# S5 local response from Toeplitz tables spread by one-hot matmuls, 28 adaLN weight tiles moved to VectorE, z from turned u on

## The chip, the cores and the metric

The kernel runs on one core of one Trainium2 chip. Its engines run side by side, each with its own queue in order: TensorE (PE: matmul, with PEld for its weight loads), VectorE (DVE), ScalarE (ACT), GpSimd (POOL) and SyncE (SP), which issues most DMAs. The metric is the device time of one execution in microseconds. Before the change three runs gave a median of 1373.99 us (1372.52 to 1379.91).

## The reference, cut to what matters

The program is a decoder trunk of two layers on 256 tokens of width 2048. Layer 0 is an S5 state-space layer, layer 1 a native-sparse-attention layer on shared keys and values. Each layer is normalised and modulated by shift, scale and gate that come from a vector c (adaLN).

```python
c_act = jax.nn.silu(c)
shift, scale, gate = jnp.split(c_act @ mod_w[layer] + mod_b[layer], 3, axis=-1)
h = modulate(rmsnorm(x, norm_g[layer]), shift, scale)
# S5 mixer, 128 groups of 16 channels and 64 complex states
u, z = jnp.split(h @ w_in, 2, axis=-1)
x_t = a * x_{t-1} + bb @ u_t            # diagonal, complex, over 256 steps
y = Re(c @ x) + d_skip * u
y = gelu(y); y = y * sigmoid(y @ w_glu + b_glu)
out = (y * silu(z)) @ w_out
```

The scan is done in blocks of 4 steps. What a step of a block gives to later steps of the same block (four 16x16 matrices per group, K_0 to K_3, and the d_skip diagonal) is the local response; what crosses blocks goes through the states.

## The kernel before

Everything stays transposed, with channels on the 128 partitions. A projection of one 128-column block reads 1 MB of weights in two tiles of 512 KB (ring of 8 buffers, `raw`). ACT rounds four 128-column pieces at a time to a high part (`hi`, L203), DVE takes the low part by subtraction (`lo`, L204), and PE makes three 256-column matmuls for each piece (L228 to L230): 48 to a block.

adaLN columns are made in two ways. A PE pair (`pe_mod_pair`, L158 and L163) takes two 128-column blocks with 32 matmuls of 32 output rows and a small sum; `dve_mod` (L145) takes one block as two 512 KB tiles, each by one DVE multiply with accumulate of 128x1024, against `cact`, the row silu(c) laid on all partitions. `PE_MODS` and `DVE_MODS` say which columns go where: 32 to PE, 64 to DVE (beside 32 for the first shift and scale, always on PE).

The program runs in stages:

- the first norm, half of u (L299 to L302) with the first adaLN columns, and, on DVE, the discretised tables of the S5 layer;
- the S5 stage, in halves f = 0 and 1 of the groups: `u_turn` (L544) brings u from channel order to group order, `scan_in` (L597) forms the block inputs, `scan_run` (L622 to L644) runs the scan on DVE, `scan_out` (L657) forms the outputs from the states, `y_turn` turns back (L672) and adds the local response (L679) by 32x32 matmuls with `kd`, then ACT takes the gelu. u's second half and z are projected meanwhile. z overwrites x0, which holds u until y_turn has read it (the assert in `z_half`);
- glu and w_out, then the second norm (hkv), the projections of keys and values with the compressed blocks, the rows of q;
- 16 attention heads, each with its z, w_o, and the last norm.

Every call of `fill()` takes the next entry of the table `PLAN`; its letters say what is put there: u or z half blocks (`u`, `z`), a PE pair (`m`), a DVE column (`d`), compressed pieces and q rows (`c`, `q`). A scheduler then orders each engine's instructions by its own estimate of times.

Of the kernel before, what the change touches and what calls it, by code (L numbers as in the profile page):

```python
# [46 lines left out]
def spread(n, slots, a=0):  # L47
# [25 lines left out]
def trunk_kernel(ctx, tc, xT, crow, ccol, vec, m0n, mn, mt, w_ur, w_in, w_glu, w_out, w_kv, w_qr, w_q, w_g,  # L73
# [49 lines left out]
    kd = ey[:, 0:2048].rearrange("p (m d c) -> p m d c", m=16, d=4)  # L123
# [10 lines left out]
    modw = pool.tile([128, 80], F32, name="modw")  # L134
# [3 lines left out]
    def dve_mod(n=1):  # L138
        for i in range(ndve[0], min(ndve[0] + n, len(DVE_MODS))):
            col = DVE_MODS[i]  # L140
            for e in range(2):
# [5 lines left out]
                                               accum_out=modw[:, col - 48:col - 47] if e else modv[:, col:col + 1])  # L147
# [280 lines left out]
    V.tensor_reduce(par, id32.rearrange("p (e c) -> p e c", e=2), axis=AX.X, op=OP.add)  # L428

# [16 lines left out]
    for s in (2, 3, 0, 1):  # L446
# [14 lines left out]
        bb = [ey[:, 2112 + 256 * r:2368 + 256 * r] for r in range(2)]  # L461
# [61 lines left out]
    powers()  # L523
    pick = stab[:, 832:1104]
# [27 lines left out]

    ustate, zstate, ydone = [0, None], [0, None], [0]
# [12 lines left out]
    def z_half():  # L566
# [3 lines left out]
        assert m < 8 * ydone[0]  # L570
# [74 lines left out]

    def scan_out(f, cts):

        VH = VV[f]
        for q in range(2):
# [10 lines left out]
            for g2 in range(2):  # L660
                nc.scalar.activation(U[:, 8 * f + 4 * q:8 * f + 4 * q + 4, 2 * g2:2 * g2 + 2, :], p[g2], AF.Copy)
# [4 lines left out]
    def y_turn(f):  # L666

        for mp in range(4 * f, 4 * f + 4):
            p = psb([128, 2, 8, 4, 8], "yt")
            for j in range(4):  # L670
                for g in range(4):
                    nc.tensor.matmul(p[32 * g:32 * g + 32, :, :, j, :], turn[:, 32 * j:32 * j + 32],  # L672
                                     U[:, 2 * mp:2 * mp + 2, g, :].rearrange("p m (i s) -> p m i s", i=8),
                                     start=(j == 0), stop=False, skip_group_check=True)
            for ml in range(2):
                for d in range(4):
                    for g in range(4):
                        pr = slice(32 * g, 32 * g + 32)
# [12 lines left out]
    for q in range(4):  # L691
        fill()
# [449 lines left out]
```

## Time and profile before

| | us |
|---|---|
| median of three runs | 1373.99 |
| profiled execution | 1384.57 |
| its span, first to last instruction | 1382.9 |
| PE busy in it | 1286.8 |
| DVE busy in it | 1021.4 |
| ACT busy in it | 678.4 |
| S5 stage, from the first `ut` matmul (165.3) to the first glu matmul (437.5) | 272.2 |
| glu and w_out (437.5 to 631.5) | 194.0 |

The trace is one execution, slower by 0.8% than the median of the runs. Matmul ends are modelled, so two starts in a row tell a matmul's price better than its duration does. An idle engine costs something only where another waits for it.

### The profile page before, as it was taken

The numbers are of one execution on the slowest core, as the hardware profiler recorded it, in microseconds if no ns is written. First come the engines' busy times: TensorE is split into PE (matmuls) and PEld (weight loads), VectorE is DVE, ScalarE is ACT, GpSimd is POOL, SyncE is SP. The second block draws the span as 40 slices with busy tenths as digits, with TensorE's granted clock in tenths as the row PEclk, the third lists the DMA queues.
The fourth block names the chain that finished last, engine by engine and source line by source line (L and its number), as shares of the span: only waits on it lengthen the run. The fifth ranks groups of instructions, "written<-read, shape, count | busy, mean of one in ns | idle before, by whom it ended". The sixth has DMA issues, their size and how long they took to land.

```text
span 1382.9 us, 32898 instructions
## 1 busy us (share of the span) xinstructions
PE 1286.8 (93%) x13194; PEld 1222.9 (88%) x13194; DVE 1021.4 (74%) x2228; ACT 678.4 (49%) x1473; POOL 18.2 (1%) x44
## 2 busy tenths in 40 slices
PE   2799999889999999996999899999999999999995
PEld 1688798879889999995899899999999999999995
DVE  5998649874246888878997787777878777777665
ACT  3345543244345555543554545554565555555653
POOL 2000000000010000000000000000000000000000
PEclk9789999889999999997999999999999999999998
DMA  9798856669577899876788788876556444445541
GB/s 338 267 361 302 309 182 246 235 256 335 182 272 249 300 326 332 308 243 221 258 317 279 253 265 271 300 265 226 182 182 209 152 146 150 153 138 167 178 160 61
DMA packets 93258, 331.13 MB, mean 239 GB/s; under 512 B 12512, under 2 KB 12672, under 8 KB 92080
## 3 DMA queue, kind: packets, MB, share of 16 engines
q1 hardware_dynamic: 91792, 321.45, 67.4%
q0 software_dynamic: 1312, 7.58, 1.5%
q8 instruction: 103, 1.69, 0.5%
q14 instruction: 51, 0.42, 0.1%
HBM read 324.79 MB, written 4.19 MB: 238 GB/s over the span
## 4 chain that ended last, share of the span: by engine, by line
PE 74%; DVE 11%; DMA 11%; issue 2%; ACT 2%; SPq 0%; DVEq 0%; ACTq 0%
PE acc L230 19%; PE acc L228 18%; PE acc L229 18%; DMA raw<-in_mt_dram 8%; DVE lo L204 3%; PE macc L158 3%; DMA raw<-in_w_in_dram 2%; PE yt L679 1%; DVE raw L145 1%; PE s L976 1%; DMA mraw<-in_m0n_dram 1%; PE vp L597 1%; PE ut L544 1%; PE op L1027 1%; PE kp L473 1%
## 5 line engine op out<-in xcount | busy, mean ns | idle before, releaser
L203 ACT ACTIVATE hi<-raw 128x512 fp32r<-128x512 f32 x640 | 399.3, 630 | 425.7 <-PE acc L229 352.6
L204 DVE TENSOR_TENSOR lo<-raw,hi 128x512 fp32r<-128x512 f32 x640 | 431.8, 688 | 188.5 <-ACT hi L203 172.4
L229 PE MATMUL acc<-hq,hi 128*128 128x256 f32 x960 | 274.6, 286 | 0.0
L228 PE MATMUL acc<-hq,hi 128*128 128x256 f32 x960 | 272.9, 284 | 0.4 <-ACT hi L203 0.4
L230 PE MATMUL acc<-hq,lo 128*128 128x256 f32 x960 | 271.0, 284 | 1.8 <-DVE lo L204 1.7
L145 DVE SCALAR_TENSOR_TENSOR raw<-raw,cact 128x1024 f32<-128x1024 f32 x128 | 156.3, 1221 | 64.5 <-DMA raw<-in_mt_dram 64.3
L229 PEld LDWEIGHTS acc<-hq,hi 128*128 128x128 f32 x960 | 180.8, 188 | 3.7 <-issue 3.3
L230 PEld LDWEIGHTS acc<-hq,lo 128*128 128x128 f32 x960 | 180.3, 188 | 4.3 <-DVE lo L204 2.9
L228 PEld LDWEIGHTS acc<-hq,hi 128*128 128x128 f32 x960 | 180.9, 188 | 1.3 <-issue 0.7
L230 PE MATMUL acc<-hkv,lo 128*128 128x256 f32 x384 | 113.5, 297 | 4.1 <-DVE lo L204 3.9
L228 PE MATMUL acc<-hkv,hi 128*128 128x256 f32 x384 | 112.3, 294 | 3.5 <-ACT hkv L262 3.4
L229 PE MATMUL acc<-hkv,hi 128*128 128x256 f32 x384 | 111.2, 292 | 3.7 <-DVE hkv L263 3.7
L230 PE MATMUL acc<-h,lo 128*128 128x256 f32 x384 | 109.1, 284 | 0.2 <-DVE lo L204 0.2
L228 PE MATMUL acc<-h,hi 128*128 128x256 f32 x384 | 109.2, 284 | 0.0
L229 PE MATMUL acc<-h,hi 128*128 128x256 f32 x384 | 108.2, 282 | 0.0
L158 PE MATMUL macc<-mraw,cz 128*32 128x128 f32 x2048 | 73.1, 299 | 24.8 <-DMA mraw<-in_m0n_dram 20.1
L158 PEld LDWEIGHTS macc<-mraw,cz 128*32 128x32 f32 x2048 | 60.6, 120 | 31.7 <-issue 20.0
L230 PEld LDWEIGHTS acc<-hkv,lo 128*128 128x128 f32 x384 | 76.5, 200 | 6.3 <-DVE lo L204 6.0
L228 PEld LDWEIGHTS acc<-hkv,hi 128*128 128x128 f32 x384 | 76.7, 200 | 4.8 <-ACT hkv L262 4.6
L229 PEld LDWEIGHTS acc<-hkv,hi 128*128 128x128 f32 x384 | 76.3, 199 | 4.4 <-DVE hkv L263 4.3
L230 PE MATMUL acc<-yhl,lo 128*128 128x256 f32 x256 | 73.2, 288 | 3.4 <-DVE lo L204 3.2
L230 PE MATMUL acc<-ghl,lo 128*128 128x256 f32 x256 | 72.2, 283 | 3.3 <-DVE lo L204 3.3
(324 smaller groups left out, 2831.4 us busy)
## 6 DMA issues: line engine op xcount, KB each, us to landing
raw<-in_mt_dram SPq DMA_DIRECT2D x128, 512.0 KB, 5.4
raw<-in_w_z_dram SPq DMA_DIRECT2D x96, 512.0 KB, 3.6
mraw<-in_m0n_dram SPq DMA_DIRECT2D x64, 512.0 KB, 8.1
mraw<-in_mn_dram SPq DMA_DIRECT2D x64, 512.0 KB, 6.8
raw<-in_w_in_dram SPq DMA_DIRECT2D x48, 512.0 KB, 7.7
raw<-in_w_kv_dram SPq DMA_DIRECT2D x48, 512.0 KB, 5.4
raw<-in_w_glu_dram SPq DMA_DIRECT2D x32, 512.0 KB, 6.0
raw<-in_w_out_dram SPq DMA_DIRECT2D x32, 512.0 KB, 5.6
```

What stands on the lines that cost most here:

```text
L145: nc.vector.scalar_tensor_tensor(out=rf, in0=rf, scalar=1.0, in1=cact[:, 1024 * e:1024 * e + 1024], op0=OP.mult, op1=OP.mult, accum_out=mo ...
L158: nc.tensor.matmul(acc[32 * j:32 * j + 32, 128 * e:128 * e + 128], cz[:, q, :], r[:, q % 8, :], start=(e == 0 and q < 4), stop=(q >= 12), ...
L203: nc.scalar.activation(hi[:, 0:c, :], rr, AF.Copy)
L204: nc.vector.tensor_sub(lo[:, 0:c, :], rr, hi[:, 0:c, :].bitcast(F32))
L228: nc.tensor.matmul(acc, hi[:, kk, :], act(0, k), start=(k == 0), stop=False)
L229: nc.tensor.matmul(acc, hi[:, kk, :], act(1, k), start=False, stop=False)
L230: nc.tensor.matmul(acc, lo[:, kk, :], act(0, k), start=False, stop=(k == KT - 1))
L473: nc.tensor.matmul(kp[o:o + 32, x].rearrange("p b m -> p (b m)"), bb[r][pr, 32 * h:32 * h + 32], kc_[pr, 2 * h:2 * h + 2, r, :], start=(x ...
L544: nc.tensor.matmul(p[o:o + 32].rearrange("p m (i s) -> p m i s", i=8), pick[:, i:i + 32], ucm[:, bs, :, j, :], start=(j % 2 == 0), stop=(j ...
L597: nc.tensor.matmul(p[e][64 * g2:64 * g2 + 64, hl, r, :], VH[pr, r, h].rearrange("p b m -> p (b m)")[:, 64 * g2:64 * g2 + 64], U[pr, 8 * f ...
L679: nc.tensor.matmul(p[pr, ml, :, d:4, :], kd[pr, 2 * mp + ml, d, :], ucm[pr, 2 * mp + ml, :, 0:4 - d, :], start=False, stop=(d == 3), skip_ ...
L976: nc.tensor.matmul(sp, qo(a, h)[:, qs], kk[:, kv, b, o:o + w], start=(i == 0), stop=(i == 2))
```

## The change

`kd` becomes `kdt`, a quarter of its size in columns: each 32 partitions hold a group pair's [K_0..K_3] as 64 columns (the ACT copies for two parities become one ACT copy and one DVE multiply-add). In the new `scan_local(f)` matmuls of K=32 and M=128 with a shifted one-hot matrix `sel` spread them to block-Toeplitz tables in PSUM, ACT copies those to `tz`, and 64x64 matmuls apply them to the group-ordered u in place (`U`). `scan_out` adds the states' part to U with DVE instead of copying with ACT; `y_turn` only turns. u in channel order is then read by `u_turn` alone, so z may begin once both halves are turned. `scan_out(0)` stands ahead of `scan_run(1)`. `cact` is loaded right after the power tables, into `ey`, over `bb`. 14 columns (28 tiles) go from `PE_MODS` to `DVE_MODS`; columns 32 to 47, the first gate, are now the first of DVE's. `PLAN` is new.

```diff
-NA, NB = 16, 0
-PE_MODS = list(range(32, 48)) + list(range(96, 96 + NA)) + L1[:NB]
-DVE_MODS = list(range(96 + NA, 128)) + L1[NB:] + list(range(80, 96))
+NA, NB = 10, 8
+PE_MODS = list(range(96, 96 + NA)) + L1[:NB]
+DVE_MODS = list(range(32, 48)) + list(range(96 + NA, 128)) + L1[NB:] + list(range(80, 96))
...
-    "uu", "uu", "muu", "uu", "muu", "uu", "muu", "uu", "m", "", "m", "",
+    "ud", "ud", "ud", "ud", "uu", "uu", "uuuud", "uuuudd", "zd", "z", "zd", "z", "z", "z", "zz", "zz",
...
-        for e in range(2):
-            nc.scalar.activation(kd[:, 4 * s:4 * s + 4, :, 16 * e:16 * e + 16], ...
+        kx = kdt[s // 2][:, 4 * (s % 2):4 * (s % 2) + 4]
+        nc.scalar.activation(kx, kp[:, :, 0], AF.Copy, scale=par[:, 0:1])
+        V.scalar_tensor_tensor(kx, in0=kp[:, :, 1], scalar=par[:, 1:2], in1=kx, op0=OP.mult, op1=OP.add)
...
     powers()
+    nc.gpsimd.dma_start(cact, crow.to_broadcast((128, D)))
+    nc.scalar.activation(cact, cact, AF.Silu)
...
-        assert m < 8 * ydone[0]
+        assert m < 8 * turned[0]
...
+    def scan_local(f):
+        bs = slice(8 * f, 8 * f + 8)
+        kt = kdt[f].rearrange("p m (d c) -> p m d c", d=4)
+        for g2 in range(2):
+            for hl in range(2):
+                pr = slice(64 * g2 + 32 * hl, 64 * g2 + 32 * hl + 32)
+                p = psb([128, 8, 4, 16], "tzp")
+                for j in range(4):
+                    nc.tensor.matmul(p[:, :, j:4, :], sel[pr, 48 - 16 * j:176 - 16 * j], kt[pr, :, 0:4 - j, :],
+                                     start=(j == 0), stop=(j == 3), skip_group_check=True)
+                nc.scalar.activation(tz[:, hl], p.rearrange("p m j c -> p m (j c)"), AF.Copy)
+            for hl in range(2):
+                p = psb([128, 8, 64], "tp")
+                for m in range(8):
+                    for e in range(2):
+                        pr = slice(64 * e, 64 * e + 64)
+                        nc.tensor.matmul(p[pr, m, :], tz[pr, hl, m, :], U[pr, 8 * f + m, 2 * g2 + hl, :],
+                                         start=(m == 0), stop=True, skip_group_check=True)
+                nc.scalar.activation(U[:, bs, 2 * g2 + hl, :], p, AF.Copy)
+            fill()
...
-                nc.scalar.activation(U[:, 8 * f + 4 * q:8 * f + 4 * q + 4, 2 * g2:2 * g2 + 2, :], p[g2], AF.Copy)
+                V.tensor_add(u, u, p[g2])
...
-            for ml in range(2):
-                for d in range(4):
-                    for g in range(4):
-                        nc.tensor.matmul(p[pr, ml, :, d:4, :], kd[pr, 2 * mp + ml, d, :], ucm[pr, 2 * mp + ml, :, 0:4 - d, :], ...
...
     scan_in(0)
     scan_run(0)
-    for q in range(4):
-        fill()
+    scan_local(0)
...
     scan_in(1)
+    scan_out(0, load_ct(0))
     scan_run(1)
-    scan_out(0, load_ct(0))
+    scan_local(1)
     y_turn(0)
```

What PE does about the time of the second scan, before the change: outputs of the first half (`yp`, L657) between adaLN pairs (`macc`, L158 and L163), and then the turn (`yt`).

```order
L158 MATMUL macc<-mraw,cz 32x128 x32
L657 MATMUL yp_3466<-Vva,ctA 64x64 x15
L163 MATMUL macc<-ones,msum 128x1 x2
L657 MATMUL yp_3466<-Vva,ctA 64x64 x16
L158 MATMUL macc<-mraw,cz 32x128 x32
L657 MATMUL yp_3466<-Vva,ctA 64x64
```

The same place now: the outputs (L692 here) stand between half blocks of z (L228 to L230).

```order
L692 MATMUL yp_3363<-Vva,ctA 64x64 x32
L228 MATMUL acc<-h_160,hi 128x256
L229 MATMUL acc<-h_160,hi 128x256
L230 MATMUL acc<-h_160,lo 128x256
L228 MATMUL acc<-h_160,hi 128x256
```

24 projection matmuls of z follow each such pair of outputs where adaLN pairs stood; the spread matmuls of `scan_local(1)` (L668) come next, again between projections.

On DVE, the last part of the first scan (the fix-ups L643 and L644) stood alone before the change:

```order
L643 TENSOR_TENSOR scr<-scr 128x896
L644 TENSOR_TENSOR Vva<-Vva,scr 128x16x56
L643 TENSOR_TENSOR scr<-scr 128x896
L644 TENSOR_TENSOR Vva<-Vva,scr 128x16x56
L643 TENSOR_TENSOR scr<-scr 128x896
```

Now adaLN products (L145) and low parts for u's second half (L204) stand between them (L655 and L656 are the fix-ups).

```order
L655 TENSOR_TENSOR scr<-scr,stab 128x896
L204 TENSOR_TENSOR lo<-raw,hi 128x512 x2
L145 SCALAR_TENSOR_TENSOR raw,modv<-raw,ey 128x1024
L204 TENSOR_TENSOR lo<-raw,hi 128x512
L145 SCALAR_TENSOR_TENSOR raw,modw<-raw,ey 128x1024
L656 TENSOR_TENSOR Vva<-Vva,scr 128x16x56
```

Eight such products stand between the start of the first scan and u's last low part, and 13 between the start of the second scan and the last addition of L697.

On PE at the second norm (`rsum`, L250), the first projection of keys and values (`hkv`) followed at once:

```order
L230 MATMUL acc<-ghl_5721,lo 128x256
L250 MATMUL rsum<-tot,ones 128x256
L228 MATMUL acc<-hkv_8239,hi 128x256
L229 MATMUL acc<-hkv_8239,hi 128x256
L230 MATMUL acc<-hkv_8239,lo 128x256
```

Now four adaLN pairs stand about the norm.

```order
L230 MATMUL acc<-ghl_5122,lo 128x256
L158 MATMUL macc<-mraw,cz 32x128 x32
L250 MATMUL rsum<-tot,ones 128x256
L163 MATMUL macc<-ones,msum 128x1 x2
L158 MATMUL macc<-mraw,cz 32x128 x32
L163 MATMUL macc<-ones,msum 128x1 x2
```

Two more pairs follow, and then the same projection.

## Rows read from the trace of the kernel before

**Rows 1.** The page: busy time of each engine; the chain's shares.
```profile
PE 1286.8 (93%) x13194; PEld 1222.9 (88%) x13194; DVE 1021.4 (74%) x2228; ACT 678.4 (49%) x1473; POOL 18.2 (1%) x44
PE 74%; DVE 11%; DMA 11%; issue 2%; ACT 2%; SPq 0%; DVEq 0%; ACTq 0%
```

**Rows 2.** Windows by stage: length, busy by engine, granted clock, DMA share, GB/s.
```profile
165.30:197.30 32.00, 32.00 (x507) 25.86 (x507) 7.19 (x13) 14.81 (x36) 0.00 (x0) 1.00 0.47 159
...
254.10:297.40 43.30, 36.65 (x816) 31.80 (x811) 41.83 (x72) 12.65 (x31) 1.06 (x2) 0.76 0.64 233
297.40:356.80 59.40, 59.17 (x728) 56.68 (x718) 25.49 (x46) 24.46 (x53) 0.00 (x0) 1.00 0.91 336
...
165.30:437.50 272.20, 259.88 (x4125) 234.24 (x4125) 158.51 (x279) 111.91 (x243) 4.62 (x16) 0.94 0.68 239
...
437.50:631.50 194.00, 187.30 (x1538) 184.26 (x1537) 158.22 (x300) 99.06 (x179) 0.00 (x0) 1.00 0.86 302
631.50:663.00 31.50, 18.38 (x106) 15.83 (x105) 28.79 (x65) 12.10 (x26) 0.00 (x0) 0.73 0.55 186
663.00:857.00 194.00, 183.61 (x1461) 178.86 (x1461) 157.19 (x307) 95.95 (x186) 0.00 (x0) 0.96 0.82 275
```

**Rows 3.** Windows of 25 us: early, and one of projections alone.
```profile
75.00:100.00 25.00, 23.04 (x320) 19.37 (x313) 24.97 (x35) 11.06 (x26) 0.56 (x1) 0.87 1.00 384
...
575.00:600.00 25.00, 25.00 (x213) 25.00 (x212) 19.56 (x38) 12.93 (x23) 0.00 (x0) 1.00 0.76 250
```

**Rows 4.** Timeline of PE: start, duration, line, shape, instructions (two records each).
```profile
165.33 7.10 PE L544 MATMUL ut<-x,stab 128*32 128x512 f32 x64
...
194.29 1.91 PE L597 MATMUL vp<-U,Vva 64*64 64x64 f32 x64
196.12 0.39 PE L228 MATMUL acc<-h,hi 128*128 128x256 f32 x1
...
293.12 1.08 PE L672 MATMUL yt<-U,stab 128*32 128x128 f32 x32
294.13 2.38 PE L679 MATMUL yt<-x,ey 32*32 32x256 f32 x64
296.44 1.96 PE L158 MATMUL macc<-mraw,cz 128*32 128x128 f32 x64
```

**Rows 5.** The chain in order of time: outputs of the second half.
```profile
356.86 7.09 PE yp L657 x250
```

**Rows 6.** The costliest groups: adaLN on PE and on DVE.
```profile
L158 PE MATMUL macc<-mraw,cz 128*32 128x128 f32 x2048 | 73.1, 299 | 24.8 <-DMA mraw<-in_m0n_dram 20.1
L145 DVE SCALAR_TENSOR_TENSOR raw<-raw,cact 128x1024 f32<-128x1024 f32 x128 | 156.3, 1221 | 64.5 <-DMA raw<-in_mt_dram 64.3
```

**Rows 7.** Timeline of DVE: the first scan's start, two low parts, the second scan.
```profile
197.35 0.69 DVE L622 TENSOR_TENSOR scr<-Vva,scr 128x512 f32<-128x512 f32 x1 [1.72 <-ACT Vva L603]
...
199.17 0.68 DVE L204 TENSOR_TENSOR lo<-raw,hi 128x512 fp32r<-128x512 f32 x1
199.77 0.68 DVE L625 TENSOR_TENSOR Vva<-scr 128x512 f32<-128x512 f32 x1
...
254.10 0.69 DVE L622 TENSOR_TENSOR scr<-Vvb,scr 128x512 f32<-128x512 f32 x1 [4.25 <-ACT Vvb L603]
...
296.33 1.08 DVE L644 TENSOR_TENSOR Vvb<-Vvb,scr 128x896 f32<-128x896 f32 x1
```

**Rows 8.** Waits: who waited for whom, total us, times, longest.
```profile
DVE raw L145 <- DMA raw<-in_mt_dram: 64.3, 53, 4.1
```

**Rows 9.** Timeline of PE at the second norm.
```profile
631.50 0.28 PE L230 MATMUL acc<-ghl,lo 128*128 128x256 f32 x1
...
645.98 0.58 PE L229 MATMUL acc<-hkv,hi 128*128 128x256 f32 x1 [3.68 <-DVE hkv L263]
```

**Rows 10.** Timeline of DVE at the second norm.
```profile
634.41 0.48 DVE L741 SCALAR_TENSOR_TENSOR x<-acc,modv,x 128x256 f32<-128x256 f32 x1
...
644.30 1.23 DVE L145 SCALAR_TENSOR_TENSOR raw<-raw,cact 128x1024 f32<-128x1024 f32 x1 [1.99 <-DMA raw<-in_mt_dram]
...
661.26 0.87 DVE L263 SCALAR_TENSOR_TENSOR hkv<-xn,modv,hkv 128x256 fp32r<-128x256 f32 x2
```

More of the change, by code (lines that the diff above doesn't have):

```diff
@@ L122, in trunk_kernel @@
     ey = pool.tile([128, 2624], F32, tag="cact", name="ey")
-    kd = ey[:, 0:2048].rearrange("p (m d c) -> p m d c", m=16, d=4)
+    cact = ey[:, 0:2048]
     nc.vector.memset(cz, 0.0)
@@ L182, in mod_finish @@
             assert len(t) == t[-1] + 1 - t[0]
-            nc.vector.tensor_add(modv[:, c], modv[:, c], modw[:, c.start - 48:c.stop - 48])
+            nc.vector.tensor_add(modv[:, c], modv[:, c], modw[:, c.start - 32:c.stop - 32])
             nc.vector.tensor_add(modv[:, c], modv[:, c], vv_("mb", c.start, c.stop))
@@ L428, in trunk_kernel @@
     V.tensor_reduce(par, id32.rearrange("p (e c) -> p e c", e=2), axis=AX.X, op=OP.add)
+    id16 = stab[:, 1856:1872]
+    V.tensor_add(id16, id32[:, 0:16], id32[:, 16:32])
+    sel = stab[:, 640:816]
+    nc.gpsimd.memset(sel, 0.0)
+    for e in range(2):
+        nc.gpsimd.tensor_copy(sel[:, 48 + 64 * e:64 + 64 * e], id32[:, 16 * e:16 * e + 16])
+    kdt = [ey[:, 2048:2560], stab[:, 0:512]]
+    kdt = [t.rearrange("p (m n) -> p m n", m=8) for t in kdt]
     def outer(dst0, dst1, mr, mi, wr, wi, sub):
@@ L460, in trunk_kernel @@
         nc.scalar.activation(kc_[:, :, :, 16:64], ct[:, :, :, 0:48], AF.Copy)
-        bb = [ey[:, 2112 + 256 * r:2368 + 256 * r] for r in range(2)]
+        bb = [ey[:, 256 * r:256 * r + 256] for r in range(2)]
         for r in range(2):
@@ L498, in trunk_kernel @@
     mt_ = scr[:, 1536:2432].rearrange("p (g i s) -> p g i s", g=16, i=7)
-    QW = [scr[:, 2432 + 512 * i:2944 + 512 * i].rearrange("p (i g) -> p i g", i=8) for i in range(2)]
-    SG = [scr[:, 3456 + 128 * i:3584 + 128 * i].rearrange("p (r g) -> p r g", r=2) for i in range(2)]
-    w1, w2_ = [scr[:, 3712 + 192 * i:3904 + 192 * i] for i in range(2)]
+    QW = [t.rearrange("p (i g) -> p i g", i=8) for t in (stab[:, 1344:1856], scr[:, 2432:2944])]
+    SG = [t.rearrange("p (r g) -> p r g", r=2) for t in (stab[:, 512:640], stab[:, 1970:2098])]
+    w1, w2_ = [scr[:, 192 * i:192 * i + 192] for i in range(2)]
+    tz = scr[:, 2944:3968].rearrange("p (l m n) -> p l m n", l=2, m=8)
     def powers():
@@ L644, in scan_run @@
                     V.tensor_tensor(x, x, mt_, op=OP.subtract if e and not r else OP.add)
+    def scan_local(f):
[12 more added lines that the diff above has]
+                for m in range(8):
+                    for e in range(2):
+                        pr = slice(64 * e, 64 * e + 64)
[3 more added lines that the diff above has]
+            fill()
     def scan_out(f, cts):
@@ L707, in trunk_kernel @@
     y_turn(1)
-    cact = pool.tile([128, D], F32, tag="cact", name="cact")
-    nc.gpsimd.dma_start(cact, crow.to_broadcast((128, D)))
-    nc.scalar.activation(cact, cact, AF.Silu)
     y_split(1)
@@ L713, in trunk_kernel @@
     n = 16 - zstate[0] // 2
-    pz = spread(PLAN[slot[0]].count("m"), n)
+    pz, dz = [spread(PLAN[slot[0]].count(c), n) for c in "md"]
     slot[0] += 1
@@ L717, in trunk_kernel @@
         z_half()
+        dve_mod(dz[m])
         z_half()
@@ L733, in trunk_kernel @@
     tot = pool.tile([128, L], F32, tag="tot", name="tot")
-    while npe[0] < 16:
-        pe_mod()
+    while ndve[0] < 16:
+        dve_mod()
+    mod_finish(32, 16)
     x = pool.tile([128, KT, L], F32, tag="cb", name="x")
@@ L746, in trunk_kernel @@
         fill()
-    while npe[0] < 16 + NA:
+    while npe[0] < NA:
         pe_mod()
-    while ndve[0] < 32 - NA:
+    while ndve[0] < 48 - NA:
         dve_mod()
```

34 lines of the change are left out of this document (15 added, 19 removed), and 9 rows, old and new, of the table PLAN.

## The prediction, made before the changed kernel was run

> **What bounds the kernel now.** I read the page first, then windows by stage, then the chain, the timelines of PE and DVE in the S5 stage and at the second norm, and the waits. The page says that PE is busy for 93% of the span and that 74% of the chain is PE [rows 1]. So what leaves PE shortens the program where PE is the one waited for, and what goes to DVE (busy 74%) is free only where DVE has room. The windows [rows 2] show where that is. In the S5 stage, 272.2 us, DVE is busy for only 158.5; PE is busy for 259.9, but at a mean clock of 0.94, and its worst stretch, under the second scan (254.1 to 297.4), has 36.7 of 43.3 busy at a clock of 0.76 while DVE is busy for 41.8. In glu and w_out both are loaded (187 and 158 of 194, DMA at 0.86). At the second norm PE is busy for 18.4 of 31.5. In the key and value stage it loses some 10 of 194.
>
> **PE's work in the S5 stage, before and after.** Prices: a projection matmul 25.00/213 = 0.117 us [rows 3]; a `ut` of 32 matmuls 7.1, a block of inputs (`vp`) 196.12 - 194.29 = 1.83, a turn 294.13 - 293.12 = 1.01, the local matmuls of two blocks of channels 296.44 - 294.13 = 2.31 [rows 4]; the outputs of a half 7.1 [rows 5]; an adaLN pair 73.1/32 = 2.28, as 2048 records are 32 pairs [rows 6]. From the first `ut` to the first glu matmul the order of before has 1117 projections, 2 `ut`, 8 `vp`, 2 outputs, 8 turns, 8 local pieces and 16 pairs: 130.7 + 14.2 + 14.6 + 14.2 + 8.1 + 18.5 + 36.5 = 236.8. The stage took 35.4 more: 12.3 idle (272.2 - 259.9), 15.6 of low clock (0.06 of 259.9), and 7.5 of changes of form and short waits.
>
> After the change the order has 1128 projections, the same `ut`, `vp`, outputs and turns, 2 pairs, no local pieces, and the new matmuls. A spread table streams 512 + 384 + 256 + 128 = 1280 columns. No row shows a matmul of 32 rows by 128 columns. The nearest is `ut`: 32 matmuls of 512 columns, four beside each other in output rows, in 7.1, so 0.89 for 512 columns in one place. That gives 2.22 for a table and 17.8 for the eight; if the two tables of a pair ran beside each other, 8.9. I take 17.8, because the order has the four matmuls of one table and then those of the other. The 128 matmuls of 64x64 that apply them are of the outputs' form: 7.1. Sum: 132.0 + 14.2 + 14.6 + 14.2 + 8.1 + 17.8 + 7.1 + 4.6 = 212.6, 24.2 less. The local response itself is not cheaper (24.9 for 18.5); the 14 pairs are the gain, 31.9.
>
> The Trainium skill, "TensorEngine Tiling (Array Packing)", Key Properties, says that different tiles of the array load and multiply in parallel, and lists the 32x128 form with four tiles. By that rule the tables would cost 8.9 and the sum would be 203.7; `vp` in rows 4 agrees for output halves, but no row here shows two row groups that feed the same output columns.
>
> **DVE paces it instead.** The 20 adaLN columns of the stage bring 40 products at 1.22 [rows 6], 49 us, that DVE did not have there. Both engines' queues are in order, so I walk through them, in us from the first `ut`. Low parts cost DVE 0.60 each (199.77 - 199.17), a scan without anything between 42.5 (254.10 to 297.4, less the y work in it) [rows 7].
> - PE ends the first inputs at 7.1 + 7.3 + 48 x 0.117 = 20.0; the scan starts 1.2 later (196.12 to 197.35) [rows 4, 7], at 21.2. Before it was 32.0.
> - DVE reaches the last low part of u after 32.6 of scan (nine fix-ups of 1.1 are left), 22 low parts (13.2) and 8 products (9.8): 76.8. PE's own work would bring it to the second `ut` at 70; it gets there at 78.2.
> - `ut`, four `vp` and 58 projections take 21.2, so the second scan starts at 100.6; before it was 88.8.
> - Up to the last addition of L697 DVE has the scan 42.5, 34 low parts 20.4, 8 additions (as long as a low part, 4.8; from 0.4 to a product's 1.22 each, 3 to 10), 16 steps on y of 256 columns (about 0.4, two thirds of a low part, 6.4) and 13 products 15.9: 90.0. The last turn on PE waits for that addition, at 190.6. What was ACT's copy and off DVE is now behind products in its queue, and PE has nothing else to do there.
> - PE then has half of the turns 4.0, 288 projections 33.7 and 2 pairs 4.6: 232.9. Low parts for these are no limit (21 low parts and 10 products, 25 us).
>
> To 232.9 I add the 7.5 of changes of form as before and 2 for the clock, which stays at 1.00 where projections stand among small matmuls (165.3 to 197.3, rows 2). The stage comes to 242, 30 less than 272.2.
>
> **The other stages.** In glu and w_out there are three more pairs, +6.8, and ten DVE products fewer (12.2 of 158). The stage loses 194.0 - 1536 x 0.117 = 14 to DVE and its loads, of which I give back 2: +5 (bounds -3 and +10). At the second norm [rows 9, 10] the last matmul ends at 631.8; L741 gets its turn 2.6 later, a product with its load takes 3.2, and the first hkv matmul that has both parts starts 14.2 later. Without products it should be about 8, in which the four pairs (9.1) run; then 16 tiles at 0.8 of DVE end at 21, with one block (5.6) done. Lost are 15.4. Before it was 31.5 less some 103 projections (12.1), 19.4: -4, and the four pairs are inside. Uncovered, they would cost 9. Key and value stage: two columns fewer, 4.9 of DVE's 157: -2 (bounds -5 and 0). Early, DVE is full (24.97 of 25, rows 3) and gets four multiply-adds of at most a low part each, 2.4: +1.5. Table loads on ACT have cover, as ACT is busy for 111.9 of 272. The 14 columns' bytes are the same on either queue. The one load of `cact` on POOL is waited for by ACT's copies of u; 96 row matmuls of u, 24 projections and a pair, 16 us of PE, lie between its release by the last `kp` matmul and the first `ut`, so I price it at nothing (uncovered, by the nearest row, a load's longest wait in rows 8: 4.1).
>
> Sum: -30 + 5 - 4 - 2 + 1.5 = -29.5. Against the profiled execution 1384.6 that is 1355; at the ratio of the runs' median to it (1373.99/1384.57) **1345**.
>
> **Rivals.** *DVE is not in the way* (its actual starts are earlier than my walk): then PE's work sets the stage, 212.6 + 7.5 + 2 = 222, -50, and the whole is -49.5: 1325. For it speaks that DVE's total fits (158.5 + 49); against it that the low parts stand behind products in one queue.
>
> *DVE waits for its loads as before.* A product waited 64.3/128 = 0.50 on average [rows 8]. The walk has 24 products (8, 2 beside the second inputs, 14 up to the turn), 12 us: 1357. For: ring of eight buffers, freed by the same DVE. Against: DMA was at 0.68 in this stage, not 0.86.
>
> *The clock stays low.* If the stage keeps the 0.76 of the second scan, PE's 49 between scan start and second `ut` become 65 for 57, the 79 up to the turn become 104 for 90, the last 42 become 56: +34, of which 2 are in the sum already, and the time is as before, 1376. Against it stands the 1.00 of 165.3 to 197.3 and of 297.4 to 356.8 [rows 2], both with projections among other work. The Trainium skill, "TensorE: Matmul & The Clock Gate", Part 1, puts the clock down to how busy PE has lately been; the 0.76 stretch with 6.7 idle agrees.
>
> *Slower:* DVE stands at the head of its queue for late loads in the scans, and low parts and additions behind it hold PE. The longest wait was 4.1 [rows 8]; at that for each of 12 columns on the walk the stage gains 49, and the time is 1373.99 + 20 = 1394. It decides from 29.5/24 = 1.2 for a product on, 2.4 times the mean of before.
>
> **How the numbers follow.** Forecast 0.58, DVE not in the way 0.13, loads 0.15, clock 0.06, slower 0.08. This kernel can tell 0.5%, some 7 us, from no change. Faster: the first two and nearly all of the third, 0.83. Same: the clock case and the rest of the third, 0.09. Slower 0.08. The forecast's own terms (5 + 8 + 7 + 3 to either side, hardly all together) are about 15. The range reaches from below the second case to between the third and the fourth: 1320 to 1370.
>
> **What would show it.** Right: the first glu matmul some 30 earlier after the first `ut`; the second scan's start later than before by about 12; PE idle ahead of the second `ut` and of the last turns, with DVE as releaser; eight tables at 2.2; a clock near 1.00 under the second scan; L145 with smaller waits; the pairs at the second norm inside PE's gap. Wrong: tables at 1.1, the second scan's start at 89 or earlier, products that wait over 1 us each, or a clock below 0.9 under the second scan.

## The result, and the profile after

The changed kernel takes 1358.33 us (median of four, 1356.18 to 1361.33) where the kernel before took 1376.95 in the same comparison: a ratio of 0.987, with a 95% interval of 0.982 to 0.991. It is 18.6 us faster; 29.5 were forecast. The time lies in the range, 13 us above the forecast.

The page of the changed kernel, busy times and the chain's shares [rows 1]: VectorE rose by 35.5 us, TensorE fell by 19.7.

```profile
PE 1267.1 (94%) x12526; PEld 1203.9 (89%) x12526; DVE 1056.9 (78%) x2291; ACT 688.1 (51%) x1463; POOL 21.7 (2%) x47
...
PE 62%; DMA 4%; DVE 3%; issue 1%; ACT 1%; DVEq 0%; ACTq 0%
```

The windows by stage, columns as in [rows 2]: first `ut` to second scan in three parts, second scan to last addition (the last L697, on which the last turn waits), the rest; then the S5 stage as a whole, glu with w_out, the second norm, keys and values.

```profile
166.30:187.90 21.60, 21.60 (x379) 16.09 (x379) 11.22 (x22) 10.45 (x26) 0.00 (x0) 1.00 0.75 251
187.90:252.20 64.30, 61.50 (x534) 53.09 (x537) 63.05 (x112) 25.85 (x47) 0.00 (x0) 0.92 0.56 192
252.20:269.40 17.20, 17.20 (x336) 15.40 (x329) 8.75 (x11) 8.85 (x24) 0.00 (x0) 1.00 0.25 76
269.40:362.50 93.10, 87.49 (x1269) 78.82 (x1267) 85.48 (x154) 48.15 (x80) 1.06 (x2) 0.97 0.59 215
362.50:412.30 49.80, 44.71 (x484) 42.55 (x485) 30.69 (x67) 20.65 (x41) 3.58 (x13) 0.95 0.77 272
166.30:412.30 246.00, 232.50 (x2993) 205.95 (x2993) 199.20 (x363) 113.94 (x215) 4.64 (x15) 0.96 0.61 214
412.30:605.20 192.90, 192.21 (x1742) 190.15 (x1740) 146.23 (x263) 100.19 (x185) 0.00 (x0) 1.00 0.88 313
605.20:636.70 31.50, 25.23 (x350) 21.80 (x350) 26.19 (x58) 16.45 (x41) 0.00 (x0) 0.78 0.95 358
636.70:829.40 192.70, 183.95 (x1488) 180.08 (x1487) 163.23 (x323) 97.14 (x186) 0.00 (x0) 0.97 0.85 294
```

Three things are to be seen. The S5 stage went from 272.2 to 246.0. From the second scan to the last addition the clock is 0.97, and 0.96 in the first 43 us of it, where the 43 us of the second scan had 0.76 before; under the first scan (187.9 to 252.2) it is 0.92. In glu and w_out TensorE has lost nearly all of its idle time (0.7 of 192.9), although three pairs more are there. Against the profile before, 28.4 us are gone from the span (1382.9 to 1354.5), 10 more than the medians say: the profiled execution of before was a long one. The comparison of stages below therefore uses two further profiles, each near its median.

VectorE's first and second scan start at 21.6 and 103.1 after the first `ut` [rows 7], the last `ut` block at 79.9:

```profile
187.90 0.69 DVE L634 TENSOR_TENSOR scr<-Vva,stab 128x512 f32<-128x512 f32 x1 [1.73 <-ACT Vva L615]
...
269.43 0.69 DVE L634 TENSOR_TENSOR scr<-Vvb,stab 128x512 f32<-128x512 f32 x1 [1.72 <-ACT Vvb L615]
```

```profile
246.23 7.10 PE L556 MATMUL ut<-x,stab 128*32 128x512 f32 x64
```

What TensorE waits for in the stage, 13.5 us in all with shorter waits, and VectorE's waits for product loads there, nine of 40 products:

```profile
PE acc L230 <- DVE lo L204: 9.3, 8, 2.4
PE yt L708 <- DVE U L697: 2.8, 1, 2.8
PE yt L708 <- issue: 1.3, 1, 1.3
```

```profile
DVE raw L145 <- DMA raw<-in_mt_dram: 20.8, 9, 4.0
```

The groups of adaLN work [rows 6]: 28 more products, and less waiting for them in all, 57.3 instead of 64.3.

```profile
L145 DVE SCALAR_TENSOR_TENSOR raw<-raw,ey 128x1024 f32<-128x1024 f32 x156 | 189.9, 1220 | 63.0 <-DMA raw<-in_mt_dram 57.3
...
L158 PE MATMUL macc<-mraw,cz 128*32 128x128 f32 x1600 | 56.5, 292 | 24.4 <-DMA mraw<-in_m0n_dram 19.8
```

### The profile page after: what moved, and what is told of

It reads as the page before. It is cut to its first block, busy times and chain, and to the rows that moved or that the text cites. A ratio compares the mean times of both kernels' runs of the same rounds, so it can differ in the third digit from the quotient of the medians.

```text
span 1354.5 us, 31620 instructions
## 1 busy us (share of the span) xinstructions
PE 1267.1 (94%) x12526; PEld 1203.9 (89%) x12526; DVE 1056.9 (78%) x2291; ACT 688.1 (51%) x1463; POOL 21.7 (2%) x47
## 4 chain that ended last, share of the span: by engine, by line
PE 62%; DMA 4%; DVE 3%; issue 1%; ACT 1%; DVEq 0%; ACTq 0%
PE acc L230 18%; PE acc L229 18%; PE acc L228 18%; DMA raw<-in_mt_dram 3%; PE s L1002 1%; DVE lo L204 1%; PE op L1053 1%; PE macc L158 1%; PE op L1050 1%; DMA raw<-in_w_kv_dram 1%; DVE raw L145 1%; PE op L1054 1%; PE cp L838 0%; PE qacc L915 0%; PE cp L839 0%
## 5 line engine op out<-in xcount | busy, mean ns | idle before, releaser
L204 DVE TENSOR_TENSOR lo<-raw,hi 128x512 fp32r<-128x512 f32 x640 | 433.2, 688 | 154.5 <-ACT hi L203 148.2
L228 PE MATMUL acc<-hq,hi 128*128 128x256 f32 x960 | 273.1, 285 | 0.4 <-ACT hi L203 0.4
L230 PE MATMUL acc<-hq,lo 128*128 128x256 f32 x960 | 271.0, 284 | 1.5 <-DVE lo L204 1.3
L145 DVE SCALAR_TENSOR_TENSOR raw<-raw,ey 128x1024 f32<-128x1024 f32 x156 | 189.9, 1220 | 63.0 <-DMA raw<-in_mt_dram 57.3
L230 PEld LDWEIGHTS acc<-hq,lo 128*128 128x128 f32 x960 | 180.4, 189 | 3.5 <-DVE lo L204 2.1
L228 PEld LDWEIGHTS acc<-hq,hi 128*128 128x128 f32 x960 | 181.0, 189 | 1.2 <-issue 0.7
L230 PE MATMUL acc<-h,lo 128*128 128x256 f32 x384 | 112.3, 294 | 9.4 <-DVE lo L204 9.3
L230 PE MATMUL acc<-hkv,lo 128*128 128x256 f32 x384 | 112.3, 293 | 4.5 <-DVE lo L204 4.3
L228 PE MATMUL acc<-hkv,hi 128*128 128x256 f32 x384 | 112.0, 292 | 0.9 <-ACT hi L203 0.9
L228 PE MATMUL acc<-h,hi 128*128 128x256 f32 x384 | 112.8, 294 | 0.0
L229 PE MATMUL acc<-h,hi 128*128 128x256 f32 x384 | 110.2, 287 | 0.0
L230 PEld LDWEIGHTS acc<-h,lo 128*128 128x128 f32 x384 | 74.5, 195 | 12.4 <-DVE lo L204 11.4
L230 PEld LDWEIGHTS acc<-hkv,lo 128*128 128x128 f32 x384 | 76.1, 198 | 6.1 <-DVE lo L204 5.8
L158 PE MATMUL macc<-mraw,cz 128*32 128x128 f32 x1600 | 56.5, 292 | 24.4 <-DMA mraw<-in_m0n_dram 19.8
L228 PEld LDWEIGHTS acc<-hkv,hi 128*128 128x128 f32 x384 | 76.4, 199 | 1.5 <-ACT hi L203 1.5
L228 PEld LDWEIGHTS acc<-h,hi 128*128 128x128 f32 x384 | 74.6, 194 | 2.9 <-issue 0.8
L229 PEld LDWEIGHTS acc<-h,hi 128*128 128x128 f32 x384 | 74.7, 195 | 0.0
```

The lines of the kernel that those rows point to most:

```text
L145: nc.vector.scalar_tensor_tensor(out=rf, in0=rf, scalar=1.0, in1=cact[:, 1024 * e:1024 * e + 1024], op0=OP.mult, op1=OP.mult, accum_out=mo ...
L158: nc.tensor.matmul(acc[32 * j:32 * j + 32, 128 * e:128 * e + 128], cz[:, q, :], r[:, q % 8, :], start=(e == 0 and q < 4), stop=(q >= 12), ...
L204: nc.vector.tensor_sub(lo[:, 0:c, :], rr, hi[:, 0:c, :].bitcast(F32))
L228: nc.tensor.matmul(acc, hi[:, kk, :], act(0, k), start=(k == 0), stop=False)
L229: nc.tensor.matmul(acc, hi[:, kk, :], act(1, k), start=False, stop=False)
L230: nc.tensor.matmul(acc, lo[:, kk, :], act(0, k), start=False, stop=(k == KT - 1))
```

## The experiments

Theory at the outset: VectorE's in-order queue of scan steps, products and low parts sets the S5 stage, as the prediction's walk has it. Rivals: the loads of the products, or TensorE's own work. The table gathers what each version's profile shows, in us from its first `ut`, and its median time. A profile is one execution: the S5 stage of unaltered code came out at 246.0, 247.4 and 244.9 (the last in "pairs out of the norm", which does not touch it), so differences of 2 or 3 us in one column say little. The kernel before has no addition; there the column holds ACT's last copy of the outputs, which the addition replaces.

| version | last ut matmul | second scan | last addition | first glu | time |
|---|---|---|---|---|---|
| before, second profile | 72.3 | 86.4 | 197.1 | 266.7 | 1376 to 1379 |
| changed, second profile | 86.6 | 103.3 | 196.2 | 247.4 | 1359.2 |
| z late | 90.6 | 99.7 | 211.1 | 260.1 | 1378.1 |
| pairs back on TensorE | 96.8 | 117.7 | 218.8 | 292.5 | 1403.6 |
| short products | 88.1 | 102.5 | 194.5 | 240.0 | 1357.4 |
| products without loads | 89.7 | 104.6 | 192.6 | 236.1 | 1350.1 |
| tables alternating | 86.1 | 102.8 | 198.5 | 252.3 | 1361.9 |
| short and alternating | 86.0 | 100.4 | 192.5 | 239.1 | 1350.8 |
| loads by GpSimd | 86.7 | 101.6 | 200.7 | 251.8 | 1365.0 |
| seven buffers | 85.4 | 100.2 | 202.5 | 250.9 | 1365.8 |
| four columns moved, alternating | 86.4 | 103.1 | 199.1 | 245.6 | 1360.6 |
| pairs out of the norm | 86.8 | 103.5 | 195.7 | 244.9 | 1361.2 |

**Both kernels again.** No edit.

> The changed kernel again, nothing altered, for a second profile and a narrower ratio. Theory (the change is worth about 27 us, nearly all of it in the S5 stage, and the kernel before merely has a wider spread from run to run, so that its profiled execution lay high): ratio 0.983 to 0.988, S5 stage again 244 to 248 us, second norm stage again 223 to 225. Rival (the change is worth the forecast 2.1%, and the first comparison caught a fast mix of runs of before): ratio below 0.982.

> The kernel before once more, for a second profile, since its profiled execution lay 0.5% above its median. Theory (the excess was in the S5 stage, where loads and pairs come out differently from run to run): S5 stage 264 to 270 us, all other stages within 1.5 us of before. Rival (the excess was elsewhere): S5 stage 271 to 274.

The changed kernel: 1359.17 against 1378.12 (17 runs of before, 1371.45 to 1384.46), ratio 0.987 (0.984 to 0.990). The theory's band holds. Windows of the second profile of before (execution 1379.7, span 1378.0; S5 stage, glu and w_out, second norm, keys and values):

```profile
162.20:428.90 266.70, 254.91 (x4126) 230.68 (x4126) 158.61 (x279) 112.07 (x243) 4.63 (x16) 0.97 0.69 243
428.90:627.60 198.70, 188.19 (x1537) 184.35 (x1536) 157.80 (x300) 99.05 (x179) 0.00 (x0) 1.00 0.85 294
627.60:659.00 31.40, 18.60 (x104) 16.26 (x103) 28.99 (x64) 11.98 (x25) 0.00 (x0) 0.67 0.55 189
659.00:851.00 192.00, 180.48 (x1463) 175.87 (x1463) 157.04 (x307) 96.93 (x186) 0.00 (x0) 0.98 0.82 277
```

and of the changed kernel (execution 1360.46, span 1358.7):

```profile
166.60:414.00 247.40, 234.39 (x2994) 207.81 (x2994) 200.17 (x365) 113.91 (x216) 5.09 (x15) 0.95 0.61 215
414.00:608.20 194.20, 192.35 (x1741) 190.08 (x1740) 145.47 (x262) 99.85 (x185) 0.00 (x0) 1.00 0.88 310
608.20:639.70 31.50, 25.80 (x363) 22.24 (x362) 27.66 (x63) 17.16 (x42) 0.00 (x0) 0.84 0.94 361
639.70:832.60 192.90, 182.49 (x1476) 177.46 (x1475) 161.59 (x319) 96.55 (x185) 0.00 (x0) 0.98 0.85 294
```

Between these two the span falls by 19.3: up to the first `ut` +4.4, S5 stage -19.3, glu and w_out -4.5, norm, keys and values +1.0, the rest -0.9. The stage of before was 5.5 shorter than in the profile that the prediction used, as the theory had it; that all other stages agree within 1.5 was wrong: glu and w_out differ by 4.7, the part ahead of the first `ut` by 3.1, keys and values by 2.0. In the stage itself TensorE had the same matmuls in both profiles; it was busy for 259.9 at a mean clock of 0.94 in the first and for 254.9 at 0.97 in the second, so nearly all of the 5.5 is a lower clock in the first.

**Early z undone.**

```
-"zd", "z", "zd", "z", "z", "z", "zz", "zz", "zz", ... "zz",
+"d",  "",  "d",  "",  "",  "",  "",   "",   "",  ... "zzzzzzzzzzzzzzzzzzzz",
```

> Undoes the early z alone: the twenty half blocks of z between the second inputs and the last y turn of the first half stand behind that turn, as in the kernel before. Theory (VectorE paces the stage, and z only has to be somewhere under the second scan): the second scan starts about 5 us sooner, TensorE has less between the small matmuls, the stage is 238 to 246 and the time 0 to 8 us lower. Rival (z early is what keeps TensorE busy and its clock up under the second scan, and part of the gain): the granted clock there falls below 0.9 and the stage grows by 5 to 15 us.

1378.12, ratio to before 1.000 (0.998 to 1.002): all of the gain is gone. The rival holds: the stage is 12.7 longer and the clock falls below 0.9. The time grows by 19, of which 3.6 are in glu and w_out. From the second scan to the last addition, the changed kernel (second profile), then this one:

```profile
269.90:362.80 92.90, 87.75 (x1269) 78.90 (x1267) 84.81 (x151) 47.86 (x80) 1.05 (x2) 0.98 0.60 214
```

```profile
268.00:379.40 111.40, 98.27 (x1270) 88.41 (x1266) 91.33 (x159) 41.76 (x79) 1.06 (x2) 0.88 0.54 188
```

For the same matmuls TensorE is busy 10.5 longer, at the lower clock, and idle 8.0 longer. The trace shows the place: a stretch under the second scan, then ACT and TensorE in it.

```profile
290.00:310.00 20.00, 13.97 (x113) 10.33 (x115) 19.25 (x35) 4.59 (x9) 0.00 (x0) 0.57 0.00 1
```

```profile
294.86 0.63 ACT L646 ACTIVATE Vvb<-scr 128x512 f32<-128x512 f32 x1 [17.76 <-DVE scr L637]
295.40 0.58 ACT L670 ACTIVATE scr<-tzp 128x512 f32<-128x512 f32 x1
```

```profile
296.03 1.98 PE L676 MATMUL tp<-U,scr 64*64 64x64 f32 x32 [8.36 <-ACT scr L670]
297.93 7.78 PE L668 MATMUL tzp<-stab 32*128 32x512 f32 x16
```

ACT's copy of the carries waits 17.8 for the scan, the copy of a table stands behind it in ACT's queue, and TensorE waits 8.4 for that copy with nothing else to do. After this idle time the granted clock is 0.50, the lower of its two levels (1.2 GHz), over the next pair of tables, which takes 7.78 instead of 4.03. Nothing is loaded meanwhile: SyncE's queue holds a load of z weights that waited 56.1 for a buffer, until a low part gave one back:

```profile
SPq L191 <- DVE lo L204: 102.9, 21, 56.1
```

This version is not the order of before in this place: there adaLN pairs stood among the outputs, and here nothing does, since the pairs have gone to VectorE. So it shows what an empty place costs there; whether other work than z would fill it as well was not run.

**The move of the tiles undone.** The lists, loops and adaLN entries of before, with sixteen pairs among the new S5 slots:

```
-NA, NB = 10, 8
+NA, NB = 16, 0
-"ud", "ud", "ud", "ud", "uu", "uu", "uuuud", "uuuudd", "zd", "z", "zd", "z", "z", ...
+"u", "u", "u", "u", "uum", "uum", "uuuum", "uuuu", "zm", "z", "zm", "z", "zm", ...
```

> Undoes the move of the tiles alone: the sixteen pairs (one to three in each part of the S5 stage, sixteen there in all) are back on TensorE and the products leave VectorE there; tables and early z stay, the later stages are as in the kernel before. Theory (in the changed kernel TensorE is nearly full in the S5 stage, so 14 pairs at 2.1 to 2.3 come on top, less the 10 us that VectorE and its loads cost): stage 260 to 268 instead of 247, time 1371 to 1379, nearly that of the kernel before; neither early z nor the move is worth much without the other. Rival (early z is the gain, the move is a wash): stage 244 to 251, time 1355 to 1364.

1403.63, ratio to before 1.019 (1.016 to 1.022), 25 us beyond the theory's band: tables and early z without the move are slower than before. Against the changed kernel the stage is 45.1 longer, the part ahead of it 6.0 longer, and glu with w_out 10.2 shorter. Of the 45.1, TensorE is busy for 33.1 more (267.5 for 234.4), near the 31.9 of fourteen pairs at 2.28, and idle for 12.0 more; behind the last addition (391.4 to 465.1) ACT waits for weights, which share SyncE's queue with the pairs' tiles:

```profile
ACT hi L203 <- DMA raw<-in_w_in_dram: 32.0, 6, 7.7
```

**Short products, and products without loads.**

```
+w = 32 if i < 20 else 1024        # short: in0, in1 and out over w columns
+if i >= 20: dma_start(r, ...)     # without loads: in0 is cact for i < 20
```

> Leaves out part of the sums of the first 20 adaLN columns on VectorE (each product covers 32 of 1024 elements; all loads stay). Theory (VectorE's in-order queue of products and low parts sets the S5 stage): 40 products of 1.22 become about 0.1, the stage falls from 246 to between 222 and 232, the time by 14 to 24 us to about 1338. Rival 1 (the loads of the products set it: a product at the head of the queue waits for its load whatever its length): the stage loses under 8 us. Rival 2 (TensorE sets it): the stage stays at 244 to 248.

> Leaves the weights out of the first 20 adaLN columns on VectorE: their 40 products have full length but multiply a resident tile, so their 40 loads of 512 KB are gone from SyncE's queue. Theory (VectorE's own time sets the stage and the loads only its end): the 5.2 us wait before the last addition and some of the 15 us of waits behind it go, the stage falls by 5 to 10 us, the time to about 1350. Rival 1 (loads set it): 15 us or more. Rival 2 (TensorE sets it): under 2 us.

Short: 1357.35, ratio 0.984 (0.981 to 0.988); without loads: 1350.06, 0.981 (0.978 to 0.984). The S5 stage of the one, then of the other:

```profile
168.50:408.50 240.00, 231.19 (x2993) 207.03 (x2993) 160.80 (x356) 113.07 (x216) 4.52 (x15) 0.95 0.61 219
```

```profile
165.10:401.20 236.10, 232.15 (x2994) 204.79 (x2994) 202.96 (x371) 111.13 (x214) 4.57 (x15) 0.97 0.46 156
```

39 us of VectorE's work gone bring the stage 7.4 and the time 1.8, less than its runs spread (1349.2 to 1360.5); without their loads the same products bring the stage 11.3 and the time 9.1. Neither moves the second `ut` forward. My theory falls: VectorE's busy time is not what sets the stage. In the first version the first rival's bound (under 8) held. In the second the time came out as the theory had it, and the stage between the theory's 5 to 10 and the rival's 15. TensorE, idle for 13.0 in the changed kernel's stage, is idle for 8.8 in the one and for 3.9 in the other, all of that ahead of the second scan. So about 236 is what this order takes with TensorE full. Which of the things that go with the 40 loads counts (their bytes, their buffers, their place in the queue) this run does not tell.

**Tables alternating**, alone and with short products.

```
-for hl in range(2):
-    for j in range(4): matmul(p[:, :, j:4, :], sel[pr, ...], ...)
+for j in range(4):
+    for hl in range(2): matmul(tp_[hl][:, :, j:4, :], sel[pr, ...], ...)
```

> The matmuls of the two spread tables of a pair alternate, so that two tiles of 32 rows that feed the same 128 output columns stand next to each other. Theory (no two of them run beside each other; a pair of tables takes 4.0 as it does now): a pair stays at 4.0 and the time within 2 us of 1359. Rival (tiles of different row groups multiply side by side): a pair takes 2.0 to 2.4, TensorE has 7 us less, the second ut comes 3 to 4 us earlier and the time falls by 4 to 8.

> Both reliefs at once: the products of the first 20 columns cover 32 of 1024 elements (part of their sums is left out), and the matmuls of the two spread tables alternate. Theory (up to the second ut, TensorE with its lost clock and VectorE's queue arrive at the same time, so that lifting one of them alone shows the other): the last ut matmul comes 80 to 84 after the first instead of 86 to 88, the stage takes 228 to 236, the time is 1344 to 1352. Rival (the loads of the products and the weights, which both versions keep, set the stage): ut within 1 of 87, the stage 238 to 242, the time within 3 us of the 1357 of the version with short products alone.

Alone: 1361.85, ratio 0.990 (0.987 to 0.994); its profiled execution lay 0.9% above its median, so its stage in the table may be long. With short products: 1350.84, 0.980 (0.977 to 0.982). A pair of tables in the changed kernel and in the alternating one:

```profile
189.72 4.03 PE L668 MATMUL tzp<-ey,stab 32*128 32x512 f32 x16
```

```profile
192.09 2.42 PE L667 MATMUL tzp<-ey,stab 32*128 32x512 f32 x16
```

The theory was wrong on the tables: alternated, the two run largely beside each other, and the order of the changed kernel gave that away. The Trainium skill, "TensorEngine Tiling (Array Packing)", Key Properties, says that different tiles can load weights and multiply in parallel; the 2.42 agrees. The theory was right that nothing comes of it: TensorE's busy time falls by 7.4, the time does not. With short products the second `ut` still comes at 86.0 and the stage takes 239.1, as the rival said; only the time, 6.5 below short products alone, is what the theory asked, and 4.4 of that lie in keys and values, which the edit does not touch. TensorE then has 4.5 us less to do up to that point and waits 6.7 there for low parts, where the changed kernel waits 2.8. VectorE in turn waits up to there for ACT's high parts (13.1) and for product loads (6.1). So TensorE and VectorE arriving together are not the whole reason; a version with alternating tables and without the loads was not run.

**The buffers and the queue of the loads.**

```
-ring = ctx.enter_context(tc.tile_pool(name="ring", bufs=8))
+ring = ctx.enter_context(tc.tile_pool(name="ring", bufs=7))
```

```
+(nc.gpsimd if i < 20 else nc.sync).dma_start(r, mt[i]...)
```

> The changed kernel with seven instead of eight buffers in the ring of raw tiles, all else equal. Theory (under the scans a buffer comes free only when VectorE reaches its low part or product, loads stop for want of buffers, and the missing weights come in a burst later): the stage grows by 5 to 12 us, with lower DMA shares in the fix-up stretches, and the other loaded stages by some as well, the time by 8 to 25. Rival (eight buffers are more than enough, the engines' own work sets the stage): stage 244 to 249, time within 3 us of 1359.

> The 40 product loads of the S5 stage go through GpSimd's queue instead of SyncE's; same buffers, same bytes. Theory (the products' loads cost because SyncE's queue is in order: a product load that waits for a buffer holds back the weights of u and z behind it): VectorE's waits for loads fall from 20 us to under 10, the stage to 238 to 243, the time by 4 to 8. Rival 1 (the eight shared buffers or the bytes decide, not the queue): stage 245 to 249, time within 2 us. Rival 2 (loads through GpSimd's queue are slower): stage over 250.

Seven buffers: 1365.76, 0.990 (0.988 to 0.992), 6.6 more than eight, and the stage 3.5 longer; up to the second scan nothing is lost, and from there to the last addition it takes 102.3 instead of 92.9. By GpSimd's queue: 1365.02, 0.992 (0.989 to 0.995), the stage over 250 as its second rival said; VectorE's waits for loads are 18.7 there, where the changed kernel has 20.8 and 22.0 and the theory asked for under 10. So buffers matter under the second scan, less than I wrote, and separating the queues does not help. Waits of SyncE's queue in the S5 stage of the changed kernel:

```profile
SPq L191 <- DVE lo L204: 86.8, 24, 10.7
SPq L143 <- DVE lo L204: 34.1, 14, 10.8
SPq L191 <- DVE raw L145: 16.7, 16, 1.7
SPq L143 <- DVE raw L145: 16.1, 14, 1.9
```

For 154 of 247 us the next load waits until VectorE gives a buffer back. A queue that loads ahead may wait at no cost, and the same queue waited as long in the kernel before (154 of 272 us in its four longest lines, for low parts and for the ends of pairs). So this says only that loads run no faster than buffers come back, and not what that costs.

**Four columns out of the end of the second scan**, with alternating tables.

```
-"zd", "z", "zd", "z", ... "d", "d", "d", "", "d", "", "d",   glu: "d", "", "d", "d", "",
+"zd", "zd", "zd", "zd", ... "", "", "", "", "", "", "d",     glu: "d", "d", "d", "d", "d",
```

> The changed kernel with alternating tables, and four adaLN columns taken out of the end of the second scan: two to the second inputs, where VectorE has room, two to the glu blocks. Theory (products at the head of VectorE's queue that wait for late loads stand before the last addition and cost 4 to 5 us): last addition 190 to 193 after the first ut instead of 196, stage 239 to 244, time 1352 to 1357. Rival (the time goes back into glu, or the last turn waits for other work): 1359 to 1363.

1360.58, ratio 0.987 (0.985 to 0.989): no gain, so the rival's band. But the edit did not do what it should: 8 products instead of 13 stand between the second scan's start and the last addition, and yet two of them stand directly ahead of the last two additions. VectorE's end of the second scan in the changed kernel (second profile), then here:

```profile
356.37 1.27 DVE L697 TENSOR_TENSOR U<-U,yp 128x512 f32<-128x512 f32 x2
361.66 1.23 DVE L145 SCALAR_TENSOR_TENSOR raw<-raw,ey 128x1024 f32<-128x1024 f32 x1 [4.01 <-DMA raw<-in_mt_dram]
362.81 0.08 DVE L145 DVE_READ_ACCUMULATOR raw<-raw,ey 128x1 f32 x1
362.81 0.68 DVE L697 TENSOR_TENSOR U<-U,yp 128x512 f32<-128x512 f32 x1
```

```profile
360.17 1.23 DVE L145 SCALAR_TENSOR_TENSOR raw<-raw,ey 128x1024 f32<-128x1024 f32 x1 [5.12 <-DMA raw<-in_mt_dram]
...
361.32 0.68 DVE L697 TENSOR_TENSOR U<-U,yp 128x512 f32<-128x512 f32 x1
364.79 1.23 DVE L145 SCALAR_TENSOR_TENSOR raw<-raw,ey 128x1024 f32<-128x1024 f32 x1 [2.78 <-DMA raw<-in_mt_dram]
...
365.94 0.68 DVE L697 TENSOR_TENSOR U<-U,yp 128x512 f32<-128x512 f32 x1
```

A product with a late load stands before the last addition in both, for 4.0 there and twice, 7.9 together, here. That it costs the last turn this wait is read from the trace; its removal alone was not tried. Without any of the 40 loads the stretch from the second scan to the last addition takes 88.0 instead of 92.9.

**Pairs out of the second norm.**

```
-"mmmm", "d", "d", "d", "d", "dcd", "dc", "cd",
+"", "dm", "d", "dm", "d", "dmcd", "dc", "mcd",
```

> The four adaLN pairs at the second norm stand between the key and value blocks instead, so the loads of w_kv no longer queue behind 8 MB of tiles. Theory (those loads are what fills the gap and took the 4 us that were forecast): from the last w_out matmul to the first on hkv 8 to 11 us instead of 17.4 to 18.9; the key and value stage gets up to 9 us of pairs; the time within 3 us of 1359. Rival (the normalisation itself on VectorE and ScalarE sets the gap): 16 us or more, and the time 5 to 9 us higher.

1361.22, ratio 0.989 (0.987 to 0.992). From the last w_out matmul to the first on `hkv` 10.9 instead of 17.4; keys and values 217.0 instead of 207.0. The theory holds for the gap: in the changed kernel it is full of the pairs' loads. SyncE's queue, TensorE and ACT there:

```profile
592.54 20.16 SPq L156 DMA_DIRECT2D mraw<-in_mn_dram  x12
613.82 1.17 SPq L191 DMA_DIRECT2D raw<-in_w_kv_dram  x2
```

```profile
620.76 1.08 PE L158 MATMUL macc<-mraw,cz 128*32 128x128 f32 x16 [1.60 <-DMA mraw<-in_mn_dram]
```

```profile
623.31 1.15 ACT L203 ACTIVATE hi<-raw 128x512 fp32r<-128x512 f32 x2 [3.16 <-DMA raw<-in_w_kv_dram]
```

None of these versions is faster than the changed kernel and still computes everything.

## Why the prediction was right or wrong

**S5 stage, -30: right in sign, too large.** 242 were forecast, a gain of 30.2; it is 26.2 against the profile that the sum was made on and 19.3 between profiles near the medians. 5.5 of the 10.9 missing are in the stage of before: I scaled the sum by the ratio of the median to the profiled execution, 0.8%, which takes 0.2 us off a gain, while the excess of that execution lay in the one stage that the change shortens, as lower clock. The other 5.4 are the difference of terms that were wrong in both directions. To TensorE's own 212.6 the prediction adds 20.3 of waiting (its walk ends at 232.9), 7.5 for changes of form and short waits, and 2 for the clock. In the second profile TensorE is idle for 13.0, and by the prediction's own way of counting the low clock costs 11.7 (0.05 of 234.4; 9.3 in the first profile), which leaves 10 for changes of form. So the clock was the term that was put too low, by 7 to 10, and TensorE's waiting was put too high by 7; that 242 came within 6 of the measured stage owes something to luck. The clock stayed up under the second scan, as the prediction said, but it was 0.92 under the first scan and 0.95 or 0.90 behind the last addition. Why it fell there is open.

**The walk on VectorE: numbers right, reason wrong up to the second `ut`.** First scan 21.2 forecast and 21.6 measured, second `ut` 78.2 and 80, second scan 100.6 and 103. In the walk TensorE could be at the second `ut` at 70 and waits 8.2 for VectorE. In the changed kernel TensorE is idle for 2.8 of that way; its own work took the rest, at a clock of 0.94: of the 10 us beyond 70, about 5 are low clock (0.08 of the 61.5 busy in the second window above). VectorE waited there 0.6 us for product loads. So the step that failed is that VectorE's queue brings TensorE to the second `ut`, and the agreement of the starts is luck. With TensorE as full as that, neither shorter products nor absent loads could bring the point forward by more than 2.8. What sets it when the tables alternate as well stays open.

**Products' loads, put at nothing.** Behind the start of the second scan the walk's order of waits is right: TensorE waits for low parts and for the last addition. But the walk has no wait for a load in it, and with the loads gone TensorE's 10.2 us of idle time from there on are gone too, while 39 us of products taken away leave 5.7. That is the third rival, which I had put at 12 us and a chance of 0.15; the stage gained 11.3 and the time 9.1 without the loads. The rival's mechanism was even waits of 0.5 at 24 products; measured were 22.0 us at nine of 40 products in the second profile, 14 of them behind the last addition. That the time it gave, 1357, is where the kernel came out is in part luck, as the clock's term has its share in the same miss.

**"The 14 pairs are the gain, 31.9": on TensorE alone, yes.** With the pairs back TensorE is busy for 33.1 more in the stage; the time rises by 44.5, as waits and the part ahead of the stage add to that and glu gives 10.2 back. But with the early z taken away the same move brings nothing. The prediction had no term for early z of its own; it stands in the clock, which the sum lets fall from 15.6 to 2. Taken away, it costs 19: it keeps TensorE supplied while ACT and VectorE are in the scan. The clock rival, 1376 and a chance of 0.06, gives the time of the kernel without it, though there the clock is 0.92 over the stage and not 0.76.

**Glu and w_out, +5: not seen.** -1.1 and -4.5 between the two pairs of profiles, but the sign can't be told: the stage took 191.3 to 197.8 in ten profiles of versions with the same work in it, and 194.0, 198.7 and, with the pairs back, 184.0 in those with three pairs less. TensorE's busy time rose by 4.2 in the second profile (192.35 of 194.2), and its idle time fell from 10.5 to 1.9, so the three pairs (6.8) stand in what were stalls. The term that was mis-sized is the 2 of 14 that fewer products give back.

**Second norm, -4, and keys and values, -2: together +1.0**, and -1.3 between the first two profiles; neither gain shows. The norm did start sooner on VectorE (first `hkv` low part 6.6 after the last w_out matmul). I priced the four pairs by their matmuls, 9.1, and not by their 8 MB, for which SyncE's queue took over 20 us. But with the pairs out of the gap the two stages together took 3.5 longer in the profile, and the time did not fall.

**Early, +1.5**: +1.0 between the first two profiles, +4.4 between the later ones; the first `ut` came between 165.1 and 170.0 in versions with the same early work, so its size can't be told.

**Tables, 17.8:** 4.03 a pair gives 16.1. The order argument was right.

## What to carry to other kernels

When work moves from one engine to another in a stage that also runs through a ring of load buffers, price the moved work's loads, and who gives their buffers back, before its busy time: here 39 us of VectorE's time were worth 7 us of the stage and no time clear of the spread, the loads alone 11 of the stage and 9 of the time. Where a start comes out as forecast, look also whether the engine that was to wait did wait: here it was busy. An edit that looks like a detail (work that may begin early) can be the condition of the whole gain, so undo each part alone. And where executions of the kernel before spread by 1%, compare stages from two profiles before forecasting a difference of 2%.

## What was not expected of the hardware

Two tables of 32 rows that feed the same 128 output columns take 4.03 us one after the other and 2.42 when their matmuls alternate. At a granted clock of 0.50 such a pair took 7.78. With the same loads through GpSimd's queue the stage was 4.4 longer, and the time 5.9. Two executions of the kernel before, with the same matmuls, had a granted clock of 0.94 and 0.97 in the S5 stage, worth 5.0 us of TensorE's busy time.
